# Four pairs instead of two in the long w_down passes, six residues by accumulating DMA, other orders and another rule for loading pairs

## The chip, the core and the metric

The kernel runs on one core of a Trainium2 chip. Its engines run side by side and wait for each other by semaphores: the tensor engine (PE, with its weight loads PEld), VectorE (DVE), ScalarE (ACT), GpSimd (POOL) and SyncE (SP). SP and POOL issue DMA transfers, and each engine takes its instructions in program order. The metric is the device time of one execution in microseconds.

## What is computed

One layer of a hybrid block on 256 rows of 2048 columns, all in float32. The part that matters is the second half, SwiGLU:

```
hn = rms_norm(h, norm2_g)                       # 256 x 2048
a  = hn @ w_gate                                # 256 x 5632
bu = hn @ w_up                                  # 256 x 5632
h  = h + (silu(a) * bu) @ w_down                # 256 x 2048
```

Before it come an input projection, attention, a convolution and an output projection, which the change does not touch.

## The kernel before

**Three products for one.** A float32 product is made of reduced-precision (float32r) ones. Each operand is split into a rounded part ("hi") and a residue ("lo"); a product then takes three matmuls: hi·hi, lo·hi and hi·lo. For a weight tile ACT makes the rounded part (`whi`, line 320) and DVE the residue (`wlo`, line 329). A residue can also be made "by DMA": ACT writes the negated rounded value into `wlo` (line 323), and a DMA issued by POOL adds the raw tile to it (line 324).

**Plain units and pairs.** The hidden width of 5632 is eleven blocks of 512 columns, in groups of 4, 4 and 3 (`FGROUPS`). After the gate and up projections of a group comes its part of the w_down product: a pass over the group's k-tiles (a k-tile is 128 rows of w_down, four to a block) in two halves of 1024 output columns. The work of a half is a list of units, run in the order of a string (`DORDERS`):

- "g" and "u" are plain units: two k-tiles by 512 columns, for both halves of the 256 rows, 12 matmuls (`multiply_two`, lines 1014, 1015, 1020). "g" takes the first 512 columns of the half, "u" the second.
- "s" is a pair unit: k-tile p of the group's first block with k-tile p of its second block, by all 1024 columns. It is a 2x2 block product by seven products instead of eight (Strassen-Winograd), 21 matmuls (`multiply_pair`, lines 993 to 995). It replaces 24 matmuls of plain units.

A pair costs more preparation: DVE forms four sums of the loaded weights (`wt`, lines 966 to 968), ACT rounds the seven matrices (`wh`, lines 969 and 972), and DVE makes their residues (`wlb`, line 975, of the loaded ones; `wlt`, line 976, of the sums). The activations need sums and residues as well (`make_down_forms`), made in between while later blocks run. Before the change two of the four k-tiles of the first two blocks go as pairs (`ND = 2`), in all three groups. The gate and up projections are built of the same units; in each of their blocks four pairs and eight plain units, some of these with the residue by DMA (`BY_DMA`).

**What sets the order.** Nothing is scheduled by a planner: the order of the emitted program is the order on each engine. `run_chunks` walks over all units; at unit t it emits the residues of units up to t + 2, then the loads of pairs that lie up to 6 units ahead (`PAIR_AHEAD`), then the loads and casts of the units up to t + 3 (near a pair) or t + 2, and then the matmuls of t. Generators that were started earlier (transposes, forms, the sums of finished products) go one step further at each `resume()`. All loads are issued by SP, so a load that waits for its buffer holds back every load behind it. Buffers: five for raw tiles (`raw`), three each for `whi` and `wlo`, two for a pair's loaded weights (`wb`), two each for `wh`, `wlb` and `wlt`, one for `wt`. A special rule held for the first four pairs, those of the first gate/up block that has any ("block 1"):

```
behind = [k for k in range(n) if chunks[k].get("kind") == "s"][NS]
...
if p < behind and p > t + hi_lead:
    break
```

So these were loaded no more than three units ahead. The two `wb` buffers hold, until then, the normalized activations `hn`, from which the forms of the gate and up projections are made.

Of the kernel before, what the change touches and what calls it, by code (L numbers as in the profile page):

```python
# [12 lines left out]
F32 = mybir.dt.float32  # L13
# [82 lines left out]

HI_AHEAD, LO_AHEAD = 3, 2

PAIR_AHEAD = 6

FIRSTS = [sum(FGROUPS[: g + 1]) for g in range(len(FGROUPS))]

# [20 lines left out]
def tile_block(  # L123
# [697 lines left out]
    def transposed(j, aa):  # L821
        last = j + 1 in FIRSTS
        b = j - group_of(j)[1]
        for t in range(N // P // 2):

            pool_, tag = (acc_ps, "acc") if last else (aux_ps, "aux")
            pt = pool_.tile([P, 2, S], F32, tag=tag, name="ps_a")
            for i in range(2):
                for m in range(NM):
                    c = (2 * t + i) * P  # L830
                    pe.transpose(pt[:, i, m * P : (m + 1) * P], aa[m][:, c : c + P], ident)  # L831
            if b < 2 and 2 * t < ND:
# [12 lines left out]
            yield from lag(1 if last else 4)  # L845
# [11 lines left out]

    def make_down_forms(g):

        fp = ffn["pool"]  # L860
        gap = lambda: lag(5 if FGROUPS[g] == 4 else 2)
        a11, a21 = (raw_act[0][:, :, m * P : (m + 1) * P] for m in range(NM))
        a12, a22 = (raw_act[1][:, :, m * P : (m + 1) * P] for m in range(NM))

        hi = fp.tile([P, 7, ND, P], F32R, tag="dhi", name="dhi")
        lo = fp.tile([P, 3, ND, P], F32R, tag="dlo", name="dlo")
        fa, fb = (lhs.tile([P, 2, ND, P], F32, tag=t, name="dsums") for t in ("lhi", "llo"))
        act.copy(hi[:, 0], a11)
        dve.scalar_tensor_tensor(fa[:, 0], a21, -1.0, a22, ALU.mult, ALU.subtract)
        yield from gap()  # L870
        act.copy(hi[:, 1], a12)
        dve.scalar_tensor_tensor(fa[:, 1], fa[:, 0], -1.0, a11, ALU.mult, ALU.subtract)
        yield from gap()
        act.activation(hi[:, 2], a22, AF.Copy, scale=-1.0)
        dve.tensor_tensor(fb[:, 0], a11, a21, ALU.subtract)
        yield from gap()
        act.copy(hi[:, 3:5], fa)
        dve.tensor_tensor(fb[:, 1], a12, fa[:, 1], ALU.subtract)
        yield from gap()
        act.copy(hi[:, 5:7], fb)  # L880
        for i, a in ((0, a11), (1, a12)):
            dve.tensor_tensor(lo[:, i], a, hi[:, i].bitcast(F32), ALU.subtract)
            yield from gap()
        dve.scalar_tensor_tensor(lo[:, 2], a22, -1.0, hi[:, 2].bitcast(F32), ALU.mult, ALU.subtract)
        yield from gap()
        pairs = [lhs.tile([P, 2, ND, P], F32R, tag=t, name="dlo2") for t in ("lhi", "llo")]
        for i, f in ((0, fa), (1, fb)):
            dve.tensor_tensor(pairs[i], f, hi[:, 3 + 2 * i : 5 + 2 * i].bitcast(F32), ALU.subtract)
            yield from gap()
        los = [lo[:, 0], lo[:, 1], lo[:, 2], pairs[0][:, 0], pairs[0][:, 1], pairs[1][:, 0], pairs[1][:, 1]]  # L890
        down_forms[g] = {f: (hi[:, i], los[i]) for i, f in enumerate((0, 1, 3, 4, 5, 6, 2))}

    forms = {}
# [176 lines left out]

    def down_pass(g, j0, nb):
        k0 = j0 * HD
        ks = [k for k in range(nb * HD) if k >= 2 * HD or k % HD >= ND]
        twos = [dict(ks=(k0 + a, k0 + b), rows=slice(k0 + a, k0 + b + 1, b - a), k=None)
                for a, b in zip(ks[::2], ks[1::2])]
        for i, order in enumerate(DORDERS[nb]):
            n = 2 * i
            end = {}  # L1080
            fast_block(order, [dict(p=p, rows=slice(k0 + p, k0 + p + HD + 1, HD)) for p in range(ND)], twos,
                       dict(g=(w_down, n * N), u=(w_down, (n + 1) * N)),
                       dict(pairs=lambda: down_forms.get(g), plain=actT.get),
                       lambda sums, n=n, end=end: down_half(g, n, sums, end),
                       lambda sums, n=n, end=end: down_whole(g, n, sums, end))

    halfway = {}

# [158 lines left out]
```

## Time and profile before

| | |
|---|---|
| median of 3 runs | 1048.9 us (1048.76 to 1049.65) |
| the profiled execution | 1048.92 us |
| its span, first to last instruction | 1047.1 us |
| granted clock of the tensor engine | 1.0 |
| first group: w_down pass, first half | 517.1 to 560.3 us |
| first group: w_down pass, second half | 560.3 to 602.5 us |
| second group: w_down pass | 768.7 to 854.2 us |
| block 1 (first block with pairs) | 390.9 to 433.6 us |

The page gives busy times by engine. A matmul's record is longer than the distance to the next one, so rates are read from starts. In a row of groups the number after the bar is the busy time, then the mean in ns, then the idle time of the engine just before these instructions and what ended it. A row "A <- B: x, n, m" of the waits says that A waited for B for x us in total, n times, m us at most. In a timeline row stand start, length, engine, line, operation, tiles, shape and count; SPq is SP's queue of DMA issues, and its length runs to the end of the last issue of the row.

### The profile page before, as it was taken

How to read it: one execution, taken by the hardware profiler on the slowest of the kernel's cores; microseconds unless marked ns; L12 is line 12 of the kernel's file. 1: busy time of each engine (PE TensorE's matmuls, PEld its weight loads, DVE VectorE, ACT ScalarE, POOL GpSimd, SP SyncE). 2: the span in 40 equal slices, each digit the busy share in tenths (PEclk: the TensorE clock that was granted, in tenths of full speed). 3: DMA queues.
4: the chain of work that ended last, by engine and by line, in shares of the span. 5: the costliest groups of instructions: out<-in, count | busy, mean ns of one | idle time of the engine just before them, and what ended most of it. 6: DMA issues, size and time to landing. Idle time of an engine off the chain costs nothing.

```text
span 1047.1 us, 12933 instructions
## 1 busy us (share of the span) xinstructions
PE 1036.2 (99%) x4663; PEld 852.5 (81%) x4663; DVE 900.6 (86%) x1095; ACT 621.6 (59%) x786; POOL 100.5 (10%) x143
## 2 busy tenths in 40 slices
PE   9999999999999999999999999999999999999998
PEld 7888887877788788888888888888888888888886
DVE  7899889898765599999787898999878789989897
ACT  7544666755756565776463657666644446657442
POOL 0130122201100100000001010000000110000010
PEclk9999999999999999999999999999999999999999
DMA  9657654453546566987867789879757879798683
GB/s 335 227 182 280 212 163 167 154 181 134 177 153 226 194 223 214 268 266 236 232 210 188 217 271 273 256 217 285 248 175 241 219 208 291 222 287 267 187 265 85
DMA packets 113936, 231.30 MB, mean 221 GB/s; under 512 B 7504, under 2 KB 8656, under 8 KB 113616
## 3 DMA queue, kind: packets, MB, share of 16 engines
q1 hardware_dynamic: 104864, 203.71, 56.9%
q0 software_dynamic: 8864, 26.74, 13.4%
q8 instruction: 36, 0.59, 0.2%
q14 instruction: 28, 0.23, 0.1%
q10 hardware_dynamic: 144, 0.03, 0.0%
HBM read 204.24 MB, written 9.44 MB: 204 GB/s over the span
## 4 chain that ended last, share of the span: by engine, by line
PE 61%; DMA 2%; DVE 2%; issue 1%; ACT 0%; DVEq 0%; POOLq 0%
PE q L1020 12%; PE q L1014 12%; PE q L1015 12%; PE q L995 8%; PE q L993 7%; PE q L994 7%; DMA raw<-in_w_down_dram 1%; PE ps_a L831 1%; DMA wlo<-raw 1%; PE acc L365 1%; PE acc L359 1%; PE acc L360 1%; DVE wlo L329 1%; DVE wlt L976 0%; DVE wt L966 0%
## 5 line engine op out<-in xcount | busy, mean ns | idle before, releaser
L320 ACT CAST whi<-raw 128x1024 fp32r<-128x1024 f32 (+1 forms) x273 | 281.5, 1048 | 141.6 <-PE acc L360 58.9
L329 DVE TENSOR_TENSOR wlo<-raw,whi 128x1024 fp32r<-128x1024 f32 (+1 forms) x239 | 287.8, 1218 | 73.5 <-ACT whi L320 73.3
L972 ACT CAST wh<-wt 128x2048 fp32r<-128x2048 f32 x52 | 99.6, 1914 | 77.6 <-DVE wt L968 76.9
L976 DVE TENSOR_TENSOR wlt<-wt,wh 128x2048 fp32r<-128x2048 f32 x52 | 119.1, 2290 | 14.9 <-ACT wh L972 14.7
L359 PE MATMUL acc<-whi,xhi 128*128 128x512 f32 x320 | 126.9, 397 | 1.0 <-ACT whi L320 0.9
L360 PE MATMUL acc<-whi,xlo 128*128 128x512 f32 x320 | 125.2, 391 | 0.0
L1014 PE MATMUL q<-whi,chi 128*128 128x512 f32 x320 | 125.2, 391 | 0.0
L1015 PE MATMUL q<-whi,clo 128*128 128x512 f32 x320 | 124.5, 389 | 0.0
L993 PE MATMUL q<-wh,fhi 128*128 128x512 f32 x280 | 109.9, 393 | 0.0
L994 PE MATMUL q<-wh,flo 128*128 128x512 f32 x280 | 109.1, 390 | 0.0
L517 DVE SCALAR_TENSOR_TENSOR y<-upad,cw,y 128x256 f32<-128x256 f32 x240 | 102.2, 482 | 2.2 <-ACT y L510 2.2
L1014 PE MATMUL q<-whi,ahi 128*128 128x512 f32 x256 | 100.2, 391 | 0.0
L1015 PE MATMUL q<-whi,alo 128*128 128x512 f32 x256 | 99.6, 389 | 0.0
L975 DVE TENSOR_TENSOR wlb<-wb,wh 128x1536 fp32r<-128x1536 f32 x52 | 91.1, 1752 | 1.8 <-ACT wh L969 1.8
L365 PE MATMUL acc<-wlo,xhi 128*128 128x512 f32 x320 | 87.8, 396 | 2.0 <-DVE wlo L329 2.0
L1020 PE MATMUL q<-wlo,chi 128*128 128x512 f32 x320 | 85.7, 390 | 0.2 <-DMA wlo<-raw 0.2
L969 ACT CAST wh<-wb 128x1536 fp32r<-128x1536 f32 x52 | 76.6, 1474 | 0.0
L365 PEld LDWEIGHTS acc<-wlo,xhi 128*128 128x128 f32 x320 | 59.7, 189 | 15.3 <-DVE wlo L329 3.3
L359 PEld LDWEIGHTS acc<-whi,xhi 128*128 128x128 f32 x320 | 60.4, 189 | 14.3 <-ACT whi L320 1.9
L1020 PEld LDWEIGHTS q<-wlo,chi 128*128 128x128 f32 x320 | 59.9, 188 | 13.2 <-DMA wlo<-raw 0.8
L360 PEld LDWEIGHTS acc<-whi,xlo 128*128 128x128 f32 x320 | 60.4, 189 | 12.2
L1014 PEld LDWEIGHTS q<-whi,chi 128*128 128x128 f32 x320 | 60.1, 188 | 12.3
(230 smaller groups left out, 1739.1 us busy)
## 6 DMA issues: line engine op xcount, KB each, us to landing
raw<-in_w_in_dram SPq DMA_DIRECT2D x79, 512.0 KB, 4.6
raw<-in_w_down_dram SPq DMA_DIRECT2D x64, 512.0 KB, 7.2
raw<-in_w_gate_dram SPq DMA_DIRECT2D x48, 512.0 KB, 7.5
raw<-in_w_up_dram SPq DMA_DIRECT2D x48, 512.0 KB, 6.2
wb<-in_w_up_dram SPq DMA_DIRECT2D x40, 512.0 KB, 3.7
wb<-in_w_gate_dram SPq DMA_DIRECT2D x40, 512.0 KB, 4.9
wlo<-raw POOLq DMA_DIRECT2D x34, 512.0 KB, 7.1
raw<-in_w_out_dram SPq DMA_DIRECT2D x32, 512.0 KB, 4.2
```

Source lines behind the costliest of these rows:

```text
L320: act.copy(c["hi"], c["raw"])
L329: dve.tensor_tensor(c["lo"], c["raw"], c["hi"].bitcast(F32), ALU.subtract)
L359: pe.matmul(ps[m], xhi[:, ms], hi[:, j, :], start=c["first"] and j == 0, stop=False)
L360: pe.matmul(ps[m], xlo[:, ms], hi[:, j, :], start=False, stop=False)
L365: pe.matmul(ps[m], xhi[:, ms], lo[:, j, :], start=False, stop=c["last"] and j == nk - 1)
L517: dve.scalar_tensor_tensor(y[:, ct, :], src, wk, y[:, ct, :], ALU.mult, ALU.add)
L976: dve.tensor_tensor(lot, c["t"], c["hi"][:, :SUMMED].bitcast(F32), ALU.subtract)
L993: pe.matmul(ps, hi, c["hi"][:, w], start=bool(first), stop=False)
L994: pe.matmul(ps, lo, c["hi"][:, w], start=False, stop=False)
L1014: pe.matmul(ps, xs[i][0][:, ms], hi[:, i, :], start=i == 0 and bool(c["first"].get(qs[m])), stop=False)
L1015: pe.matmul(ps, xs[i][1][:, ms], hi[:, i, :], start=False, stop=False)
L1020: pe.matmul(sum_bank(c, qs[m]), xs[i][0][:, ms], lo[:, i, :], start=False, stop=i == 1 and bool(c["last"].get(qs[m])))
```

## The change

In the passes of the first two groups all four pairs of the first two blocks' k-tiles are taken as pair units (`NDS = (4, 4, 2)`), so that a half has 4 pairs and 8 plain units where it had 2 and 12. Two new orders are written for them. Of the plain units, four in the first half and two in the second have their residue made by DMA. The activation forms get other buffers and are four k-tiles wide; the k-tiles 2 and 3 of the first two blocks are now kept raw for the forms instead of being split. The rule with `behind` goes; in its place the loop stops loading pairs when three lie between the current unit and the one to be loaded, for all pairs of the program. The third group keeps its orders.

```
-ND = 2
-DORDERS = {4: ("gguuggsguugsuu", "sgggugggusuuuu"), 3: ("gguusggsuu", "gggsgsuuuu")}
+NDS = (4, 4, 2)
+DORDERS = {4: ("gguusgsgsusu", "sggsggsuusuu"), 3: ("gguusggsuu", "gggsgsuuuu")}
+DOWN_BY_DMA = {4: (dict(g=(2, 3), u=(2, 3)), dict(g=(1,), u=(1,))), 3: (dict(g=(), u=()),) * 2}

-PAIR_AHEAD = 6
+PAIR_AHEAD, PAIRS = 6, 3

 def run_chunks():
-        behind = [k for k in range(n) if chunks[k].get("kind") == "s"][NS]
...
                 if chunks[p].get("kind") == "s":
-                    if p < behind and p > t + hi_lead:
+                    if sum(c.get("kind") == "s" for c in chunks[t:p]) >= PAIRS:
                         break
                     load_pair(chunks[p])

 def transposed(j, aa):
-            if b < 2 and 2 * t < ND:
-                raw_act[b] = lhs.tile([P, 2, S], F32, tag=("lhi", "llo")[b], name=f"ar{j}")
-                act.copy(raw_act[b], pt)
+            g = group_of(j)[0]
+            nd = NDS[g]
+            if b < 2 and 2 * t < nd:
+                if not b and not t:
+                    raw_act[g] = ffn["pool"].tile([P, 2, nd, S], F32, tag="draw", name="raw_act")
+                act.copy(raw_act[g][:, b, 2 * t : 2 * t + 2, :], pt)
                 yield from lag(3 if last else 6)
-                if b:
-                    start(make_down_forms(group_of(j)[0]))
+                if b and 2 * t + 2 == nd:
+                    start(make_down_forms(g))
                 continue

 def make_down_forms(g):
+        one = lambda tag, dt, name: lhs.tile([P, 4, P], dt, tag=tag, name=name)[:, :nd]
+        hi = [one("lhi", F32R, "dhi") for _ in range(4)]
+        lo = [one("llo", F32R, "dlo") for _ in range(4)]
+        f4, f5, f6, f2 = (one(t, F32, "dsums") for t in ("lhi", "lhi", "llo", "llo"))
...
+        hs = ffn["pool"].tile([P, 2, nd, P], F32R, tag="dhs", name="dhs")
...
+        ls = ffn["pool"].tile([P, 4, nd, P], F32R, tag="draw", name="dls")
+        act.copy(ls[:, 3], f6)
+        for i, (f, h) in enumerate(((f4, hs[:, 0]), (f5, hs[:, 1]), (f6, ls[:, 3]))):
+            dve.tensor_tensor(ls[:, i], f, h.bitcast(F32), ALU.subtract)

 def down_pass(g, j0, nb):
-        ks = [k for k in range(nb * HD) if k >= 2 * HD or k % HD >= ND]
-        twos = [dict(ks=(k0 + a, k0 + b), rows=slice(k0 + a, k0 + b + 1, b - a), k=None)
-                for a, b in zip(ks[::2], ks[1::2])]
+        nd = NDS[g]
+        ks = [k for k in range(nb * HD) if k >= 2 * HD or k % HD >= nd]
+        twos = [dict(ks=(k0 + a, k0 + b), rows=slice(k0 + a, k0 + b + 1, b - a), k=i)
+                for i, (a, b) in enumerate(zip(ks[::2], ks[1::2]))]
...
-                       lambda sums, n=n, end=end: down_whole(g, n, sums, end))
+                       lambda sums, n=n, end=end: down_whole(g, n, sums, end), DOWN_BY_DMA[nb][i])
```

Positions in an order string are counted from 0: in "gguusgsgsusu" the pairs stand at 4, 6, 8 and 10, and the units at 5, 7, 9 and 11 have their residue by DMA. Block 1 runs in the order "gsggsgsuusuu", before and after.

More of the change, by code (lines that the diff above doesn't have):

```diff
@@ L868, in make_down_forms @@
-        act.copy(hi[:, 0], a11)
-        dve.scalar_tensor_tensor(fa[:, 0], a21, -1.0, a22, ALU.mult, ALU.subtract)
+        raw = raw_act.pop(g)
+        a11, a21 = (raw[:, 0, :, m * P : (m + 1) * P] for m in range(NM))
+        a12, a22 = (raw[:, 1, :, m * P : (m + 1) * P] for m in range(NM))
+        one = lambda tag, dt, name: lhs.tile([P, 4, P], dt, tag=tag, name=name)[:, :nd]
+        hi = [one("lhi", F32R, "dhi") for _ in range(4)]
+        lo = [one("llo", F32R, "dlo") for _ in range(4)]
@@ L885, in make_down_forms @@
         yield from gap()
[L886 to L891, printed above, removed]
+        dve.tensor_tensor(lo[3], f2, hi[3].bitcast(F32), ALU.subtract)
@@ L1080, in down_pass @@
             end = {}
-            fast_block(order, [dict(p=p, rows=slice(k0 + p, k0 + p + HD + 1, HD)) for p in range(ND)], twos,
+            fast_block(order, [dict(p=p, rows=slice(k0 + p, k0 + p + HD + 1, HD)) for p in range(nd)], twos,
                        dict(g=(w_down, n * N), u=(w_down, (n + 1) * N)),
```

33 lines of the change are left out of this document (18 added, 15 removed).

## The prediction

> **What bounds the kernel now.** I read the page first, then the waits of the tensor engine (PE), then its timeline, and then the stages around w_down.
>
> ```profile
> span 1047.1 us, 12933 instructions
> PE 1036.2 (99%) x4663; PEld 852.5 (81%) x4663; DVE 900.6 (86%) x1095; ACT 621.6 (59%) x786; POOL 100.5 (10%) x143
> ```
> ```profile
> PE acc L365 <- DVE wlo L329: 2.0, 2, 1.2
> ...
> PE q L1020 <- DMA wlo<-raw: 0.2, 1, 0.2
> ```
>
> PE is in use almost without a break; of the rows of its waits the first shown is the largest: 2.0 us in total, 1.2 at most at a time. So the number of matmuls sets the time, as long as nothing arrives late. A matmul's shown length (0.39 us) overlaps the next one, so its price is read from starts in the timeline:
>
> ```profile
> 409.93 0.39 PE L1014 MATMUL q<-whi,chi 128*128 128x512 f32 x1
> ...
> 412.65 0.39 PE L993 MATMUL q<-wh,fhi 128*128 128x512 f32 x1
> ...
> 417.41 0.39 PE L1014 MATMUL q<-whi,chi 128*128 128x512 f32 x1
> ```
>
> At 409.93 begins a plain unit of 12 matmuls, at 412.65 a pair unit of 21. That is 2.72 / 12 and 4.76 / 21: 0.227 us for each matmul in both.
>
> The windows of two gate/up blocks and of the two w_down passes of the first group show how much room DVE has beside PE:
>
> ```profile
> 433.60:475.40 41.80, 41.80 (x190) 34.60 (x189) 39.60 (x42) 30.59 (x32) 3.44 (x4) 1.00 0.87 257
> 475.40:517.10 41.70, 41.70 (x189) 34.53 (x188) 34.42 (x37) 24.64 (x25) 2.58 (x3) 1.00 0.80 234
> 517.10:560.30 43.20, 43.20 (x195) 35.61 (x194) 37.98 (x36) 23.52 (x22) 0.00 (x0) 1.00 0.63 207
> 560.30:602.50 42.20, 42.20 (x187) 34.91 (x187) 32.96 (x33) 19.74 (x18) 5.25 (x6) 1.00 0.77 204
> ```
>
> Columns: length, then PE, weight loads, DVE, ACT, POOL busy, granted clock, DMA. PE fills every window; in the first, DVE fills 39.60 of 41.80 (95%) and PE still never waits.
>
> **Part 1: fewer matmuls.** A long pass had 2 pairs and 12 plain units, 2 x 21 + 12 x 12 = 186 matmuls; it gets 4 and 8: 180. There are four such passes (two groups, two halves), so 24 matmuls go: 24 x 0.227 = 5.4 us less on the path. The third group keeps its orders and gains nothing.
>
> **Part 2: more work on DVE and ACT.** Prices:
>
> ```profile
> 397.78 1.22 DVE L966 TENSOR_TENSOR wt<-wb 128x1024 f32<-128x1024 f32 x1
> ...
> 400.37 1.75 DVE L975 TENSOR_TENSOR wlb<-wb,wh 128x1536 fp32r<-128x1536 f32 x1
> 402.43 2.29 DVE L976 TENSOR_TENSOR wlt<-wt,wh 128x2048 fp32r<-128x2048 f32 x1 [0.31 <-ACT wh L972]
> ```
> ```profile
> L320 ACT CAST whi<-raw 128x1024 fp32r<-128x1024 f32 x271 | 280.3, 1051 | 141.2 <-PE acc L360 58.9 <-PE q L1015 42.1 <-DMA raw<-in_w_down_dram 22.7
> L329 DVE TENSOR_TENSOR wlo<-raw,whi 128x1024 fp32r<-128x1024 f32 x237 | 286.4, 1222 | 72.9 <-ACT whi L320 72.6 <-PE acc L365 0.2
> ...
> L323 ACT ACTIVATE wlo<-raw 128x1024 fp32r<-128x1024 f32 x34 | 35.9, 1055 | 0.0
> ```
>
> A pair takes DVE from 397.78 to 404.72, less 0.31 idle: 6.6 us (sums 2.6, first residue 1.75, second 2.29). A plain residue is 1.22. First half of a pass: two pairs more (13.2), eight DVE residues fewer (9.8, since four of the eight plain units left go to the DMA): 37.98 + 3.4 = 41.4 us, beside 40.8 of matmuls and 1.0 of transposes (43.20 less 186 x 0.227). Second half: six residues fewer: 32.96 + 13.2 - 7.3 = 38.9 beside 40.8, 95%, about what the window at 433.60 carried for free. The first half alone, at 99%, would not hold: at 95% it needs 43.7, 1.9 us over. Part 4 makes PE stand still for longer than that, so I charge nothing there. At the seam between the halves only one plain unit now lies between the last pair and the next one, and the bank sums of the first half stand on DVE behind that next pair's residues and one plain residue; I charge 0.75 us for each group, between 0 and 2.5 (a residue and two operations of half its size).
>
> The activation forms become 128x512 operations, half a plain residue each, about 0.6 us: eleven of them are at most 6.7 us, less what they replace, in the two blocks before the pass, which leave DVE 2.2 and 7.3 us free. Nothing on the path; if all fell into the first of these blocks, 4.5 us. Six accumulating copies for each group on POOL: it is 10% busy, and their order there is ahead of the half's writes to `hd`. ACT gets two operations for each such unit instead of one, 2.1 us, and is 59% busy. None of this is counted.
>
> **Part 3: where the loads now stand, first block.** SP issues loads in program order and stops at the first that must wait. A pair's load (L956) waits until the `wb` buffer of two pairs earlier is free, which is when DVE has written that pair's `wlb`; every raw tile behind it waits too. The trace shows both the rule and its size:
>
> ```profile
> SPq L956 <- DVE wlb L975: 336.4, 41, 13.4
> ```
> ```profile
> 361.68 10.67 SPq L315 DMA_DIRECT2D raw<-in_w_up_dram  x5
> 377.44 0.37 SPq L956 DMA_DIRECT2D wb<-in_w_up_dram  x1
> ...
> 378.41 6.40 SPq L315 DMA_DIRECT2D raw<-in_w_gate_dram  x3
> ...
> 392.10 0.37 SPq L956 DMA_DIRECT2D wb<-in_w_up_dram  x1
> ...
> 532.61 0.88 SPq L956 DMA_DIRECT2D wb<-in_w_down_dram  x2
> 533.83 16.24 SPq L315 DMA_DIRECT2D raw<-in_w_down_dram  x7
> ```
> ```profile
> 517.99 1.28 DVE L1113 TENSOR_TENSOR sum<-q,sum 128x512 f32<-128x512 f32 x2
> 519.19 1.28 DVE L1115 TENSOR_TENSOR sum<-sum,sum 128x512 f32<-128x512 f32 x2
> 520.39 2.35 DVE L329 TENSOR_TENSOR wlo<-raw,whi 128x1024 fp32r<-128x1024 f32 x2
> ...
> 530.83 1.75 DVE L975 TENSOR_TENSOR wlb<-wb,wh 128x1536 fp32r<-128x1536 f32 x1
> ```
>
> `wlb` ends at 532.58, and SP issues the two halves of the pair at 532.61 and the raw tile 1.2 us after. From a raw tile's issue to its landing, one such tile behind two pair halves took 5.5 us (issued at 601.48), another 7.4 (551.19); then the accumulating copies, near a pass and over the run:
>
> ```profile
> DMA to landing us min/median/max: 5.5/5.5/5.5
> ```
> ```profile
> DMA to landing us min/median/max: 7.4/7.4/7.4
> ```
> ```profile
> DMA to landing us min/median/max: 5.7/6.2/6.7
> ```
> ```profile
> DMA to landing us min/median/max: 5.0/7.1/10.2
> ```
>
> I take 6.4 for a raw tile, the middle of the two, and 6.2 for the copy, since few transfers run beside it at a pass's start, as in that row.
>
> Without `behind`, the loads of block 1's pairs move up in SP's queue. The first pair's load, issued at 377.44 when the second-norm forms let its buffer go, now stands ahead of the last three w_up raw tiles, which the trace issues before 372.4. They get the place of 378.41; with 5.5 the first lands at 383.9, and its cast ends at 385.0. PE wants it here:
>
> ```profile
> 382.39 0.39 PE L359 MATMUL acc<-whi,hhi 128*128 128x512 f32 x1
> ...
> 405.62 0.40 PE L995 MATMUL q<-wlt,fhi 128*128 128x512 f32 x1
> ```
>
> It is 2.6 us late. The tile at position 0 is behind the second pair's load in turn, so block 1's first `wlb`, which released SP at 392.10, comes at about 395.0 (the 2.6 and a little for the casts that are now bunched on ACT). Now the third pair's load waits for it, and behind that stands the raw tile of position 3, which the trace issued within 378.41 + 6.40. It lands at 395.0 + 1.2 + 6.4 = 402.6; cast 1.05, residue 1.22, and then the second pair's 6.9 us on DVE, in that order, end at 411.8. PE uses this `wlt` at 405.62 in the trace: 6.2 us late (5.3 to 7.2 by the two landings). PE has no slack later to win it back.
>
> **Part 4: where the loads now stand, first half of a long pass.** In "gguusgsgsusu" the pair at position 8 needs the buffer of the one at position 4, and its load stands in SP's queue right ahead of the raw tile of position 5, which is one of the tiles split by the accumulating DMA. Let T be the pass's first matmul:
>
> ```profile
> 517.11 0.39 PE L1014 MATMUL q<-whi,ahi 128*128 128x512 f32 x1
> ...
> 528.95 0.39 PE L1014 MATMUL q<-whi,ahi 128*128 128x512 f32 x1
> ```
>
> On DVE the last block's four closing operations run at 517.99 to 520.4, after PE's last matmul of that block; then come one residue (to 521.6), the sums of position 4 (to 524.2), one residue (525.3) and its `wlb` (527.0): T + 9.9. The pair's load and the raw tile follow: landing at T + 9.9 + 1.2 + 6.4 = T + 17.5. Cast and negated copy on ACT take 2.1, the accumulating copy 6.2: T + 25.8. PE, after four plain units and the transposes, starts position 4 at T + 11.8 (528.95), position 5 at T + 16.6, and its second half, which reads this residue, 8 matmuls later at T + 18.4. It stands for 7.4 us. With the ends of the rows (5.5 and 5.0; 7.4 and 7.1) 5.3 to 9.3. ACT, which waits in order for that cast, also delays the pair at position 6, but PE is late by more than that. The raw tile of position 7 follows right behind; those of 9 and 11 wait for the `wlb` of 6 and 8, which by the same steps reach PE in time now that PE is 7 us later. So the stall is paid once a pass: 2 x 7.4 = 14.8 us.
>
> For the accumulating copy, the Trainium skill ("DMA: Bandwidth & Descriptors", Anatomy of one DMA) gives 2.0 us and bytes / 436e3 us for each DMA, which would be an estimated 3.2 us for 512 KB; by it the two stalls would be 6 us shorter together and the time 1060. The trace does not agree: its quickest copy took 5.0.
>
> **Sum.** -5.4 + 6.2 + 14.8 + 1.5 = +17.1 on the profiled execution's 1048.9 (span 1047.1 and 1.8 around it, equal to the median of the three runs): 1066 us. With the low ends -5.4 + 5.3 + 10.6 + 0, 1059; with the high ones -5.4 + 7.2 + 18.6 + 5, 1074.
>
> **Rivals.** *Faster: the loads are far enough ahead.* Then only part 1 counts, 1043.5, or up to 1047 if DVE's 1.9 us in each first half show. For it: the gate/up windows hold the same mix of units without PE idle, and the first raw tile of the first pass is issued 28 us ahead of T:
>
> ```profile
> L315 SPq DMA_DIRECT2D raw<-in_w_down_dram x64: 367/368/1232, 488.7 to 1015.7; - x64
> ```
>
> Against it: the pair stands four units after the load that it blocks there, one unit here. It decides on whether position 5's tile is issued before T + 3.7 (T + 18.4 less 6.4, 2.1 and 6.2); I find it at T + 11.1. Chance 0.09.
>
> *Only one of the two late places is real.* If the passes keep up, the first block's 6.2 eats the gain: 1049.7, chance 0.04. If the first block keeps up, 1060, chance 0.06.
>
> *The standing PE loses its clock.* The first matmuls of the run are twice as far apart:
>
> ```profile
> 1.36 3.89 PE L157 MATMUL ps_warm<-ident 128*128 128x128 f32 x17 [1.36 <-POOL neghalf L151]
> ...
> 5.89 0.63 PE L359 MATMUL acc<-whi,xhi 128*128 128x512 f32 x1
> 6.32 0.63 PE L360 MATMUL acc<-whi,xlo 128*128 128x512 f32 x1
> ```
>
> 0.43 us, not 0.227, up to 5 us after PE's first work at 1.36; the granted clock is 1.00 in every window above, and the longest idle was 1.2 us. If each of the two stalls brought those 5 us at half speed back, each would cost 2.5 us more: 1071. The Trainium skill says so ("TensorE: Matmul & The Clock Gate", HAM oscillation): a gap above about 3.4 us lets the clock fall by half. No run here has such a gap yet. Chance 0.12.
>
> *The chain stays late.* If copies take the 10.2 of the worst row, positions 7 to 11 are late too, some 4 us more in each of the four halves: 1080. Chance 0.07.
>
> **How the numbers follow.** The forecast has 0.62. The range 1055 to 1075 holds its bounds, the clock case and the first-block-keeps-up case. A change of under 0.2% (2.1 us) cannot be told from none here: faster 0.09, same 0.04, slower 0.87.
>
> **What would show it.** The waits view of the new profile should have PE waiting for the copy `wlo<-raw` (second half of a plain unit) for some 5 us twice, with a shorter wait for `whi` ahead of it, and a wait for `whi` and `wlt` of together some 6 us between 380 and 415. The windows of the second halves should be near 41 us, those of the first near 49. SP's wait for `wlb` should end just ahead of position 5's raw tile. Wrong would be a PE without new waits (then the time is near 1044), or waits at the second halves (then DVE is the bound).

## The result, and the profile after

The changed kernel takes 1080.5 us (median of 4 runs, 1080.1 to 1083.1) against 1049.2 before (4 runs on the same chip, 1048.8 to 1049.7): 1.030 times as long, 95% interval 1.0286 to 1.0322. The forecast was 1066, the range 1055 to 1075: the sign was right, the size and the range were not. The profiled execution has a span of 1078.3 us, 31.2 more than before.

The page's head and first line, and the waits of PE ("A <- B: us in total, times, longest"):

```profile
span 1078.3 us, 12936 instructions
PE 1040.1 (96%) x4639; PEld 851.9 (79%) x4639; DVE 925.8 (86%) x1109; ACT 647.5 (60%) x804; POOL 112.6 (10%) x155
```
```profile
PE q L1002 <- DVE alo L844: 14.1, 2, 7.4
PE q L1029 <- DMA wlo<-raw: 6.0, 5, 2.2
PE acc L360 <- ACT whi L321: 4.0, 3, 2.6
PE q L1002 <- ACT sum L1102: 2.3, 2, 1.7
PE acc L366 <- DVE wlo L330: 2.0, 2, 1.2
PE q L1004 <- DVE wlt L985: 1.6, 3, 1.2
```

Before, the largest of these rows was 2.0 us. Now the largest is a wait of a pair's matmul (line 1002) for `alo`, the residue of an activation tile (line 844), which the forecast did not have at all; it stands 14.1 us in two stops, one for each long pass. The second row is the wait that the forecast named, but short and five times.

The windows of the first halves and second halves of the two long passes (length, busy PE, weight loads, DVE, ACT, POOL, granted clock, DMA):

```profile
523.50:577.90 54.40, 44.46 (x189) 35.31 (x187) 41.02 (x35) 30.54 (x27) 3.51 (x5) 0.94 0.70 203
577.90:620.50 42.60, 41.45 (x181) 33.60 (x182) 40.56 (x40) 23.90 (x20) 5.45 (x7) 1.00 0.90 257
786.60:842.40 55.80, 44.65 (x189) 35.42 (x187) 40.89 (x35) 30.39 (x26) 3.45 (x4) 0.94 0.70 205
842.40:885.20 42.80, 42.56 (x181) 35.11 (x182) 40.65 (x40) 24.23 (x20) 5.56 (x7) 0.96 0.88 246
```

The first halves took 43.2 us before and take 54.4 and 55.8; the second halves took 42.2 and take 42.6 and 42.8, so they lose what six matmuls fewer would give (1.4 us) and a little more. The clock, 1.00 in every window before, is 0.94 in both first halves and 0.96 in the last of these windows.

The timeline of the first pass, around the stop (T, the pass's first matmul, is at 523.50):

```profile
533.42 0.88 SPq L965 DMA_DIRECT2D wb<-in_w_down_dram  x2
...
534.35 1.33 SPq L316 DMA_DIRECT2D raw<-in_w_down_dram  x2
...
537.84 0.39 PE L1004 MATMUL q<-wlt,dhi 128*128 128x512 f32 x1
...
542.39 1.05 ACT L321 CAST whi<-raw 128x1024 fp32r<-128x1024 f32 x1 [9.84 <-DMA raw<-in_w_down_dram]
543.35 1.05 ACT L324 ACTIVATE wlo<-raw 128x1024 fp32r<-128x1024 f32 x1
544.30 0.57 ACT L842 CAST ahi<-ps_a 128x512 fp32r<-128x512 f32 x1
...
544.90 0.69 DVE L844 TENSOR_TENSOR alo<-ps_a,ahi 128x512 fp32r<-128x512 f32 x1 [6.12 <-ACT ahi L842]
...
545.65 0.80 PE L1002 MATMUL q<-wh,dhi 128*128 128x512 f32 x1 [7.42 <-DVE alo L844]
...
546.24 0.63 PE L1003 MATMUL q<-wh,dlo 128*128 128x512 f32 x1
...
546.67 0.63 PE L1004 MATMUL q<-wlb,dhi 128*128 128x512 f32 x1
```

Read from the top: SP issues the load of the pair at position 8 at 533.42, T + 9.9, and the raw tile of position 5 right behind. ACT, with nothing to do for 9.84 us, waits for this tile in order. Behind the tile's cast and negated copy in ACT's queue stands `ahi`, the rounded copy of the second transposed tile of the group's last block; only after it can DVE make `alo`, and only then is the PSUM bank of that transposed tile (`ps_a`) free. The last block's transposed tiles share a pool of banks with the sums of the pairs, and the 13th matmul of the pair at position 4 is the first into that bank. So PE stops in the middle of the pair at position 4, one unit before the place where the late tile is used. And after the stop the matmuls start 0.43 us apart (546.24, 546.67), not 0.227.

Where the 31.2 us are, from the lengths of the units in the trace: 24 matmuls fewer, -5.4; block 1 (the second block with pairs begins at 440.0, before at 433.6), +6.4; the pair at position 4, 14.2 and 13.7 us long instead of 4.9, +18.1 (stops of 7.4 and 6.6, slower matmuls 1.9 and 2.1); waits for accumulated residues at positions 7 and 11, +6.3; the first pair of the second halves (the seam), +6.0. The sum is 31.4, within 0.2 of what was measured. A unit's length here runs from the start of its first matmul to the end of its last.

### The profile page after: what moved, and what is told of

It reads as the page before. It is cut to its first block, busy times and chain, and to the rows that moved or that the text cites. A ratio compares the mean times of both kernels' runs of the same rounds, so it can differ in the third digit from the quotient of the medians.

```text
span 1078.3 us, 12936 instructions
## 1 busy us (share of the span) xinstructions
PE 1040.1 (96%) x4639; PEld 851.9 (79%) x4639; DVE 925.8 (86%) x1109; ACT 647.5 (60%) x804; POOL 112.6 (10%) x155
## 5 line engine op out<-in xcount | busy, mean ns | idle before, releaser
L321 ACT CAST whi<-raw 128x1024 fp32r<-128x1024 f32 (+1 forms) x257 | 265.7, 1050 | 148.1 <-PE acc L361 58.1
L330 DVE TENSOR_TENSOR wlo<-raw,whi 128x1024 fp32r<-128x1024 f32 (+1 forms) x211 | 255.1, 1220 | 57.5 <-ACT whi L321 56.9
L981 ACT CAST wh<-wt 128x2048 fp32r<-128x2048 f32 x60 | 115.1, 1918 | 95.5 <-DVE wt L977 95.4
L985 DVE TENSOR_TENSOR wlt<-wt,wh 128x2048 fp32r<-128x2048 f32 x60 | 137.5, 2291 | 17.7 <-ACT wh L981 17.2
L984 DVE TENSOR_TENSOR wlb<-wb,wh 128x1536 fp32r<-128x1536 f32 x60 | 105.2, 1753 | 5.2 <-ACT wh L978 5.1
L325 POOL DMA_DIRECT2D wlo<-raw x46 | 39.8, 865 | 541.8 <-ACT wlo L324 406.5
L978 ACT CAST wh<-wb 128x1536 fp32r<-128x1536 f32 x60 | 88.4, 1474 | 0.3 <-ACT wlo L324 0.2
L1023 PE MATMUL q<-whi,ahi 128*128 128x512 f32 x192 | 75.3, 392 | 0.0
L1024 PE MATMUL q<-whi,alo 128*128 128x512 f32 x192 | 74.8, 389 | 0.0
L975 DVE TENSOR_TENSOR wt<-wb 128x1024 f32<-128x1024 f32 x60 | 73.2, 1221 | 0.2
```

The lines of the kernel that those rows point to most:

```text
L321: act.copy(c["hi"], c["raw"])
L330: dve.tensor_tensor(c["lo"], c["raw"], c["hi"].bitcast(F32), ALU.subtract)
L981: act.copy(c["hi"][:, :SUMMED], c["t"])
L985: dve.tensor_tensor(lot, c["t"], c["hi"][:, :SUMMED].bitcast(F32), ALU.subtract)
L1023: pe.matmul(ps, xs[i][0][:, ms], hi[:, i, :], start=i == 0 and bool(c["first"].get(qs[m])), stop=False)
L1024: pe.matmul(ps, xs[i][1][:, ms], hi[:, i, :], start=False, stop=False)
```

## The experiments

The theory: the root is the order of SP's queue. A pair's load that must wait for its buffer stands ahead of the raw tile that is needed a unit later; that brings the first block's 6.4 us and, through ACT's queue and a PSUM bank, the stops at position 4. The rivals: the accumulating transfers are the root; the bank held by the transposed tile is the cause by itself; the pairs' work on VectorE is. All runs are listed with their times at the end of this section.

**The rule alone.** The kernel before, with the new rule for pair loads and nothing else of the change:

```
-        behind = [k for k in range(n) if chunks[k].get("kind") == "s"][NS]
...
-                    if p < behind and p > t + hi_lead:
+                    if sum(c.get("kind") == "s" for c in chunks[t:p]) >= 3:
```

> The kernel before with one edit: the rule by which a pair's load may be taken ahead is the changed kernel's (at most three pairs from the present unit on), in place of the one that held the first block's pairs back; orders, pairs and residues are those of before. Theory (the loads' order in SP's queue costs the first block its delay, the new pairs nothing there): only the first of the fast gate-and-up blocks changes, by the +6.4 us that the changed kernel shows there, so 1049.2 + 6.4 = about 1055.5, with the stop of 2.6 us near 385 us in it. Rival (that block is late by something else of the change): 1049, no stop there.

It took 1054.7 us beside 1048.2 of the kernel before on that chip: +6.4. The waits of PE in its profile:

```profile
PE acc L359 <- ACT whi L320: 3.6, 3, 2.6
PE q L994 <- DVE wlt L975: 2.0, 3, 1.6
```

These are the two waits that part 3 of the prediction named, for the cast of the last w_up tiles and for `wlt`. And the other way round, the removed rule put back into the changed kernel (beside the new one):

```
+        behind = [k for k in range(n) if chunks[k].get("kind") == "s"][NS]
...
                     if sum(c.get("kind") == "s" for c in chunks[t:p]) >= PAIRS:
                         break
+                    if p < behind and p > t + hi_lead:
+                        break
```

> The changed kernel with the removed rule put back beside PAIRS = 3: the first fast block's pairs are loaded no further ahead than in the kernel before; the passes are those of the changed kernel. Theory: the first block's 6.4 us go and the passes keep all of theirs, 1080.5 - 6.4 = 1074. Rival (the delay of that block gave loads of the passes time, so that part of it comes back there): between 1074 and 1080.

1074.6 us in one run, 5.9 less than the changed kernel (beside the kernel before on their own chips, +26.3 against +31.3, it is 5.0); the passes kept their stops (6.93 and 6.98 us inside the pair at position 4). The first block's loss belongs to the rule, and most of it adds to the rest.

**Pair loads one pair later.** The changed kernel with one number changed:

```
-PAIR_AHEAD, PAIRS = 6, 3
+PAIR_AHEAD, PAIRS = 6, 2
```

> The changed kernel with PAIRS = 2 for 3: the same products, orders and residues, and a pair's load waits in the program until only two pairs are ahead of it, which puts the load of the pair at position 8 of a long pass's first half behind the raw tiles of positions 5 and 7 in SP's queue. Theory (the head of SP's queue is the root): the stop inside the pair at position 4 and its half clock go, 9.3 and 8.8 us, and of the later waits (6.3 at positions 7 and 11, 5.8 at the seam) some or all; of the first block's 6.4 us the first 2.6 stay. So 1080.5 - 18.1 - (0 to 12.1) - (0 to 3.8) = 1046 to 1062, most likely about 1051. Rivals: if the accumulating transfers are the root, or the larger load on VectorE, little goes: 1074 or more, since neither is changed.

1058.3 us, ratio to before 1.0094 (1.0077 to 1.0111): of the 31.3 us lost 10.1 are left. The time lies in the expected range, above the likely 1051. Its waits:

```profile
PE acc L360 <- ACT whi L321: 4.5, 3, 2.6
PE q L1029 <- DMA wlo<-raw: 2.8, 3, 1.3
PE q L1002 <- DVE alo L844: 2.3, 2, 1.2
PE q L1002 <- DVE sum L1108: 2.1, 2, 1.0
```

The residues by transfer, their number, the pairs and the orders are as in the changed kernel; only the place of pair loads among the raw tiles in SP's queue differs, and the wait for `alo` falls from 14.1 to 2.3 us. This is the root of the stops. In the first block half of the loss stays (3.2 of 6.4: the second block with pairs begins at 436.8), with its 2.6 us for the cast, because the first pair's load still stands ahead of the last w_up tiles.

**The bank.** Where the transposed tiles of the last block are copied, two lags are set to 0, so that `ahi` and `alo` stand ahead of position 5's cast:

```
-            yield from lag(1 if last else 2)
+            yield from lag(0 if last else 2)
...
-            yield from lag(1 if last else 4)
+            yield from lag(0 if last else 4)
```

> The changed kernel with the two lags between the transposed tiles of a group's last block set to 0: both rounded copies of these tiles then stand on ScalarE ahead of the cast of position 5's raw tile, so their PSUM bank is free for the pair at position 4; SP's queue, orders and residues are as in the changed kernel. Theory (the raw tile's late landing is the root, the bank only where TensorE meets it): the pair at position 4 runs its 4.9 us, and position 5 then waits, about 3.2 us for its cast and 4.1 us for its residue, 7.3 together in place of the stop of 7.4; what the half clock costs (about 2 a group) may go or stay: 1076 to 1081. Rival (the bank held by the transposed tile is the cause by itself): both stops go, 2 x 9 less: 1062.

1080.8 us (one run): no change. Its waits show where the stop went:

```profile
PE q L1029 <- DMA wlo<-raw: 10.2, 6, 3.8
PE q L1023 <- ACT whi L321: 5.8, 2, 3.0
PE q L1004 <- DVE wlt L985: 5.6, 7, 1.6
```

With the bank free, PE gets through position 4 and stands at position 5 instead, 3.03 us for its cast and 2.54 for its accumulated residue in the first group, 2.79 and 3.83 in the second. The bank is only where PE met the late tile first; the rival of the bank is refuted. This kernel has the stop at the very place that the prediction gave for it.

**No accumulating transfers in the passes.**

```
-DOWN_BY_DMA = {4: (dict(g=(2, 3), u=(2, 3)), dict(g=(1,), u=(1,))), ...
+DOWN_BY_DMA = {4: (dict(g=(), u=()), dict(g=(), u=())), ...
```

> The changed kernel with all residues of the long passes on VectorE instead of six of a pass by accumulating transfer; loads and orders are unchanged. Theory: the stop inside the pair at position 4 stays in both groups (18.1 us with the clock), since nothing of SP's queue or of ScalarE's casts ahead of it is changed; the waits for accumulated residues at positions 7 and 11 (6.3 us) go, and the residues on VectorE cost between nothing and the same again: 1072 to 1082. Rival (the accumulating transfers are the root of the passes' loss): nearly all of 18.1 + 6.3 + 5.8 goes: 1052 to 1058.

1078.8 us (one run). The stop at position 4 is longer, not gone:

```profile
PE q L1002 <- DVE alo L844: 19.6, 2, 9.9
```
```profile
542.62 1.22 DVE L330 TENSOR_TENSOR wlo<-raw,whi 128x1024 fp32r<-128x1024 f32 x1 [7.52 <-ACT whi L321]
543.76 1.22 DVE L975 TENSOR_TENSOR wt<-wb 128x1024 f32<-128x1024 f32 x1
...
546.35 0.68 DVE L844 TENSOR_TENSOR alo<-ps_a,ahi 128x512 fp32r<-128x512 f32 x1
```

Position 5's residue is now on DVE, and it and the sums of the next pair stand ahead of `alo` there. The waits at positions 7 and 11 are gone, as expected. The transfers are not the root.

**Both rules, and what is left.** PAIRS = 2 with the removed rule put back (the two diffs above together) has no pair load ahead of a raw tile needed sooner:

> PAIRS = 2 and the removed rule together: no pair's load stands ahead of a raw tile needed sooner, neither in the first block nor at position 8. The run with PAIRS = 2 alone had its second fast block begin at 436.8 against 433.6 before, so 3.2 us of its 1058.3 should go: 1055.1. That leaves the passes 85.4 - 88.1 = 2.7 us slower than before in the first group, with waits of 1.2 for the transposed tile, 1.3 for position 5's residue and 1.5 at the seam. Rival: SP's queue accounts for those as well, and they go with it: 1046.

1054.6 us, ratio 1.0061 (1.0046 to 1.0076), as expected from the first block's 3.2. Yet it is 6.3 us over the kernel before, and 24 matmuls fewer should have put it 5.4 below: 11.7 us are still lost, in the passes. Its first pass and its waits:

```profile
516.50:562.50 46.00, 42.74 (x190) 34.16 (x188) 40.54 (x36) 30.60 (x27) 3.68 (x5) 1.00 0.76 218
562.50:604.90 42.40, 41.38 (x182) 33.54 (x181) 40.48 (x40) 23.68 (x19) 5.26 (x7) 1.00 0.92 263
```
```profile
PE q L1032 <- DMA wlo<-raw: 4.0, 4, 1.2
PE q L1005 <- DVE alo L847: 2.4, 2, 1.2
...
PE q L1005 <- DVE sum L1111: 2.0, 2, 1.0
```

By the lengths of the units in its trace, 3.0 of these 11.7 us are at the pair at position 4, which waits for `alo`; 5.2 at the accumulated residues of positions 5 and 7; and 3.6 at the seam. The last row names DVE for the seam, but DVE itself stands idle there, in the first pass:

```profile
559.92 1.05 ACT L321 CAST whi<-raw 128x1024 fp32r<-128x1024 f32 x1 [2.79 <-DMA raw<-in_w_down_dram]
...
561.84 0.57 ACT L1105 COPY sum<-q 128x512 f32<-128x512 f32 x1
...
562.43 0.69 DVE L1107 TENSOR_TENSOR sum<-q,sum 128x512 f32<-128x512 f32 x1 [2.79 <-ACT sum L1105]
```

ACT's copy that opens the sums of the first half (line 1105) stands behind the cast and the negated copy of the second half's first accumulated unit (position 2), and that cast waits 2.79 us for its raw tile. DVE's sums start when the copy is done, and the second half's first pair waits for them.

All further kernels are this one with one edit more each, or two. The next ones take these waits away one by one. First the lags of the transposed tiles at 0, as above:

> PAIRS = 2, the removed rule, and the two lags between the last block's transposed tiles set to 0. Now that no raw tile is late, the bank held by the transposed tile is what stops the pair at position 4 (1.2 us and about 0.3 of slower matmuls in each group): that goes, and the pair's own second residue may be late instead, as in the changed kernel with these lags at 0 (0.95 a group). 1055.1 - 3.0 + (0 to 1.9) = 1052 to 1054. Rival (VectorE is full, 40.5 us busy in a half whose matmuls take 40.8, so a wait removed is given back at the next place): 1055.

1056.1 us. The wait for `alo` is gone; in its place stand the pair's own residue (`wlt`, 0.9 us in each group) and longer waits for transfers (2.1 and 1.3 at position 5). Then, in addition, the residue of position 5 on VectorE and that of position 3 by transfer (`g=(3,), u=(1, 2, 3)`):

> As the run before, and of the four accumulated residues of a first half the one at position 5 is made on VectorE, the one at position 3 by accumulating transfer instead, so VectorE and the queues have as much to do. The wait of 1.3 and 1.2 us for position 5's transfer goes if that transfer's length is what counts: 2.5 less than the run before, about 1050. Rival (VectorE is full): the residue of position 5 is late on VectorE instead, 1052 to 1055.

1056.2 us: the transfer of position 7 is now late, by 2.0 and 2.1. Then the seam, with the first halves in another order (`"gguusgsgsusu"` to `"ggusgsgsusuu"`), without and with the lags at 0, and with the two measures before together:

> PAIRS = 2, the removed rule, and another order for the first halves, ggusgsgsusuu in place of gguusgsgsusu: each pair one position earlier, two plain units behind the last pair in place of one, so the sums of the half have 5.4 us before the second half's first pair as in the kernel before, in place of 2.7. The seam's waits (1.0 and 1.3 us, with some 0.5 of slower matmuls each) should go: 1054.6 - 3 = 1051.5. Against it: the first pair now meets the transposed tiles one unit sooner, so up to 2.7 us more there in each group, 1057.

> The order of the run before with the two lags of the transposed tiles at 0, so that their copies and residues stand ahead of the first pair's. Seam waits gone and no wait for the transposed tile: 1056.1 - 3 = 1053, down to 1050 if the pair's own residues now come in time; if VectorE is the limit and the time is only given back elsewhere, 1055 to 1056.

> The order ggusgsgsusuu with the lags at 0, and the accumulated residue of the unit behind the first pair (which was 3.0 and 2.7 us late in that run) on VectorE, a later one by transfer in its place. 1056.9 - 5.7 = 1051 if that transfer was the last wait; if VectorE is the limit, its 1.22 us make the next pair's residue late, 1054 to 1056.

1057.4, 1057.0 and 1059.8 us. In the first of them the seam's waits do go, and the second halves run in 40.8 us, which is what their 180 matmuls take (180 x 0.227). In this order the copy that opens the sums stands ahead of the accumulated unit's cast on ACT (558.96 and 562.18). But the first pair meets the transposed tiles sooner (waits of 0.42, 2.11 and 1.54 us inside it). With the lags at 0 this turns into 2.95 and 2.67 us for the transfer of the unit behind that pair, and with this residue on VectorE into waits for `wlt` and the next transfers (by the trace of an execution of 1063.2 us; the other three took 1059.7 to 1059.9). A plain unit between the two halves instead (`"sggsggsuusuu"` to `"gsggsgsuusuu"`):

> PAIRS = 2, the removed rule, and the second halves in the order gsggsgsuusuu for sggsggsuusuu: a plain unit stands between the last pair of a first half and the first of the second, 2.7 us more for VectorE there. But its first product goes to a bank that the sums free fifth of six, not first. If VectorE's load of pairs is what makes the seam late: the seam's 2.0 to 2.3 us go, 1052. If the sums' own chain is: the plain unit waits instead, about 1.5 to 3 a group, 1055 to 1058.

1063.8 us: its first product needs a bank that the sums free fifth, and waits 3.93 and 3.60 us; the rival of the sums' own chain, and more than its 1.5 to 3. Fewer and more transfers:

> PAIRS = 2 and the removed rule as before (1054.6), and all residues of the long passes on VectorE. What is left of the loss in the passes is 2.4 us at the transposed tiles, 4.0 for accumulated residues and 2.0 to 2.3 at the seams. If VectorE is the limit of the first halves (40.5 us busy, 90% and more of the stretch from position 2 to 8), four residues of 1.22 us more there and two in a second half make each pass longer by up to 7.3: 1054.6 - 4.0 + (5 to 14.6) = 1056 to 1065. If the accumulating transfers are what is left, their 4.0 go and nothing takes their place: about 1050.5.

> The other way: six of the eight residues of a first half by accumulating transfer (of the first of each stream and the rest), two fewer for VectorE, 2.4 us a half. If VectorE is the limit: between 1054.6 and 1050. If the transfers are: the two new ones are late too, or make the others so, 1056 or more.

> The same with the whole computation: PAIRS = 2, the removed rule, position 5's residue on VectorE, three transfers in a first half. The late transfer goes (1.1 and 1.2 us, with its slower matmuls 3 in all), VectorE gets 1.22 us more in each first half. If the two limits stand behind each other: 1054.6 - 3 + (2.4 to 5) = 1054 to 1056.5. If the transfer alone is the limit there: 1051.5.

1058.0 us with none, 1055.3 with six in a first half (one run) and 1057.1 with three. Each residue put back on VectorE costs time and the two transfers more gain nothing. In the last of the three the wait for `alo` is 2.33 and 2.34 us, twice what it was, since position 5's residue stands ahead of it on VectorE.

So a wait removed came back elsewhere, and often dearer: six of these nine kernels came out above every value that was expected of them (1056.1, 1056.2, 1057.0, 1059.8, 1063.8 and 1057.1). Two kernels take work off VectorE instead. In the w_down passes the residues of three of the four sums of a pair are left out (another residue of the pair is multiplied in their place, so PE has as much to do):

```
+        if c["from"]["u"][0] is w_down:
+            n = 1
+            dve.tensor_tensor(lot[:, :n], c["t"][:, :n], c["hi"][:, :n].bitcast(F32), ALU.subtract)
+            c["lo"] = [lot[:, 0]] + [lob[:, i] for i in range(3)] + [lob[:, i] for i in range(7 - SUMMED)]
+            return
```

> PAIRS = 2 and the removed rule; in the w_down passes the residues of three of the four sums of a pair are not computed (the product takes another residue of the pair in their place), so VectorE's largest operation falls from 2.29 us to about 0.7, some 6 to 8 us less in each first half and each second half; ScalarE, the transfers, the orders and TensorE's work are unchanged. If VectorE is the limit of the passes: the waits at the transposed tile, at the seam and for residues whose neighbours it held up go, 1054.6 - (6 to 10) = 1045 to 1049. If the order or the transfers are: 1052 to 1055.

1052.2 us (one run). Its first pass, and the only waits of its passes:

```profile
516.80:563.70 46.90, 43.68 (x189) 35.64 (x189) 34.99 (x39) 31.77 (x27) 4.33 (x5) 0.96 0.76 210
563.70:604.50 40.80, 40.80 (x181) 33.78 (x180) 34.27 (x37) 22.71 (x18) 4.92 (x6) 1.00 0.94 279
```
```profile
PE q L1037 <- DMA wlo<-raw: 6.6, 2, 3.4
```

The waits at the transposed tile and at the seam are gone, and the second half is at the 40.8 us of its matmuls. But now position 5's transfer alone, 3.22 and 3.40 us late with slower matmuls behind it, takes most of it back. The time falls where the rival put it (1052 to 1055), but the waits say that both have a part: with less work on VectorE `alo` is in time, and the transfer is the next limit, 2.4 us behind. For the seam this kernel shows less, since PE also reaches it later, behind the stop at position 5. Both away, that is, this kernel with position 5's residue on VectorE (`g=(3,), u=(2, 3)`):

> The run with less work on VectorE (three of the four residues of a pair's sums left out in the w_down passes), and position 5's residue of a first half on VectorE instead of by accumulating transfer. If VectorE and that transfer are all of what is left: 1052.2 - 2 x (3.3 + 1.6) = 1042.4, between 1042 and 1045, below the kernel before; that is a bound, since part of the computation is left out. If something else is left: 1048 or more.

1049.5 us, ratio 1.0013 (1.0003 to 1.0022), where 1042 to 1045 was expected. Its waits:

```profile
PE q L1037 <- DMA wlo<-raw: 3.3, 3, 1.7
PE acc L366 <- DVE wlo L330: 2.0, 2, 1.2
PE acc L360 <- ACT whi L321: 1.8, 2, 1.2
PE q L1010 <- DVE sum L1116: 1.7, 2, 0.9
PE q L1010 <- DVE alo L847: 1.5, 2, 0.7
```

The two rows on `acc` are of stages ahead of the passes. 5.1 of the 11.7 us are gone with both. Of the rest, position 7's transfer is 1.67 and 1.45 us late, and the one residue put back on VectorE, which stands there ahead of the second `alo`, is enough to make `alo` late again.

The seam's wait is not VectorE's: counted from the first pass's first matmul, the copy that opens the sums comes at 43.8 us in both of these kernels, but PE reaches the second half at 46.9 us in the first of them and at 44.8 in this one. DVE again stands idle for that copy (3.35 us), and the cast ahead of it waits 2.10 us for its raw tile.

So two limits are shown by runs: VectorE's work at the transposed tile, and the accumulating copies, which took 7.2 to 10.5 us to land in the passes of the version with 1054.6 and the first of the two kernels with less work. The third, the raw tile and the cast ahead of the sums on ACT, is read from the traces; the order `ggusgsgsusuu`, in which the copy stands ahead of that cast, had no wait for the sums, but it also has a plain unit more there. That these three are all of the 11.7 follows from the lengths in one trace and not from a run: no kernel here was without all of them. No version that computes everything beat the kernel before; the best, with 1054.6, is 0.6% slower.

All runs, in us (the kernel before had medians of 1048.1 to 1048.3 beside them):

| kernel | time | runs |
|---|---|---|
| the rule alone in the kernel before | 1054.7 | 1 |
| changed, removed rule put back | 1074.6 | 1 |
| changed, lags 0 | 1080.8 | 1 |
| changed, no transfers in the passes | 1078.8 | 1 |
| changed, PAIRS = 2 | 1058.3 | 4 |
| **PAIRS = 2 and removed rule** (all below are this with an edit) | 1054.6 | 4 |
| lags 0 | 1056.1 | 4 |
| lags 0, transfer at 3 for 5 | 1056.2 | 4 |
| order ggusgsgsusuu | 1057.4 | 4 |
| the same, lags 0 | 1057.0 | 4 |
| the same, lags 0, the early transfer later | 1059.8 | 4 |
| second halves gsggsgsuusuu | 1063.8 | 4 |
| no transfers | 1058.0 | 4 |
| six transfers in a first half | 1055.3 | 1 |
| three transfers in a first half | 1057.1 | 4 |
| fewer residues of the pairs (not the whole computation) | 1052.2 | 1 |
| the same, position 5 on VectorE (not the whole computation) | 1049.5 | 10 |

## Why the prediction was right and wrong

- **Part 1, 5.4 us for 24 matmuls: right.** A unit's length outside the stops is unchanged, and the second halves reach 40.8 us once nothing is late (shown in the runs with the other order and with less work on VectorE).
- **Part 3, the first block, 6.2: right in its place and its mechanism; the total in part by luck.** 6.4 in the trace, 6.4 by the rule alone, 5.0 to 5.9 by putting the old rule back. The 2.6 us for the late cast at 385 is in it, to the tenth. The second pair's `wlt` let PE go on at 410.70, 5.1 us behind the 405.62 of before, where 6.2 was worked out; the other 1.3 us came behind it, mostly at the next pair's residue (0.5) and at an accumulated copy (0.7), which part 3 did not have. Behind the stop of 2.6 us the matmuls were slower as well, by 1.7 us in all; as PE would have waited for that `wlt` in any case, this did not add to the 5.1.
- **Part 4, the queue: right.** SP issues the pair at position 8 at T + 9.9, and position 5's raw tile right behind, as worked out. The raw tile took 8.0 us to land, not 6.4, the copy 4.6, not 6.2; the two errors cancel, which is luck.
- **Part 4, the place of the stop: wrong.** The step that failed is the sentence on ACT, that it "also delays the pair at position 6, but PE is late by more than that". It followed ACT's queue to the next pair's casts and passed over the `ahi` that stands between, on which the bank of the pair at position 4 hangs. This moved the stop a unit forward. That its size, 7.4 and 6.6, came out near the 7.4 that was forecast is luck: the forecast's stop ended with the accumulating copy at T + 25.8, this one ends with `alo` at T + 22.1, and no copy is in it. The run with the lags at 0 shows that this is no cause of its own: the stop at position 5 costs as much.
- **The clock: wrong to leave it a rival.** A stop of 7.4 us was in the forecast itself, and the only rows on slow matmuls were those behind an idle PE. It was given a chance of 0.12; it came in both groups, at 1.9 and 2.1 us of the 2.5 charged there. The rule of the Trainium skill ("TensorE: Matmul & The Clock Gate", HAM oscillation) that was named beside that rival pointed the right way, and the trace agrees: 0.43 us between matmuls after a stop of 7.42.
- **"The stall is paid once a pass": wrong, 6.3 us.** The copies of positions 7 and 11 took 10.0 and 9.8 us to land in the first group and PE lost 1.73 and 0.94 there, 1.15 and 2.45 in the second. Part 4 took the 6.2 that was measured where few transfers ran beside them; here the DMA engines are 70% busy over the half, and 88% or more from 550 on. That this load is what made the copies longer is likely, but no run shows it alone. The rival "the chain stays late" had this step, with a chance of 0.07. That its time of 1080 is the measured one is luck: it charged some 4 us in each of four halves for the copies, where the first halves lost 2.7 and 3.6, and left out the clock and the seam.
- **The seam: 0.75 a group charged, 2.4 and 3.6 measured.** What part 2 passed over is ACT. The copy that opens the sums (line 1102) stands there behind the cast and the negated copy of the second half's first accumulated unit, and that cast waits for a late raw tile (2.19 us of idle ACT in the first group, 2.89 in the second), while DVE stands idle (3.44 and 4.14 us). The forecast looked for the delay in DVE's queue. In the second group slower matmuls are part of the 3.6. The high end of 2.5 was too low there as well.
- **Part 2, nothing charged to VectorE beside PE's own stop: hidden, not settled, by the stop.** Part 2 put a full VectorE at 1.9 us in a first half, and let the stop hide it. Without the stops the wait for `alo`, which goes when VectorE has less to do, costs 1.5 us in each first half, so this size was near. Of the other 8.8 us that the best version loses it had 1.5, the charge for the seams; the accumulated residues (5.2) and the rest of the seams (3.6 in all) it had not. For the second halves part 2's "carried for free" held: they reach 40.8 us once the seam does not wait.

In sum: 0.2 too little for the first block, 3.3 for the stops with their clock, 6.3 for the later copies and 4.5 for the seams make 14.3, within 0.2 of the 14.1 by which the forecast fell short of the profiled execution's increase. The range missed because it held either the terms at their bounds (1074) or the clock (1071), and left the later copies to a rival outside it; the runs show late tile, clock, copies and seam to come together, as one chain.

## What to carry to other kernels

When a load moves up in an in-order queue, follow what is held up through every engine's queue to the first buffer that something earlier needs; a late tile can stop the matmuls before the place where it is used. Where a second engine has nearly as much work as the first (here 40.5 us on VectorE beside 40.8 of matmuls), do not count a removed wait as gained before a run without that engine's work shows what stands behind it. When a wait names an engine that stands idle itself, follow that engine's own wait: at the seam it led from VectorE to ScalarE and to a raw tile. And where a forecast contains a stop of several us, the slower clock behind it belongs in the same term.

## What the runs showed of the hardware

The clock fell after stops much shorter than the longest forecast. Matmuls of the version with PAIRS = 2, the removed rule and the lags at 0, behind a stop of 2.09 us:

```profile
538.76 1.95 PE L1032 MATMUL q<-wlo,ahi 128*128 128x512 f32 x4 [2.09 <-DMA wlo<-raw]
540.50 0.63 PE L1005 MATMUL q<-wh,dhs 128*128 128x512 f32 x1
540.93 0.63 PE L1006 MATMUL q<-wh,dls 128*128 128x512 f32 x1
```

They start 0.43 us apart, for about 3.4 us in all. The first block of the changed kernel shows the same behind a stop of 2.60 us:

```profile
385.17 0.74 PE L360 MATMUL acc<-whi,hhi 128*128 128x512 f32 x1 [2.60 <-ACT whi L321]
385.71 0.63 PE L361 MATMUL acc<-whi,hlo 128*128 128x512 f32 x1
386.14 0.63 PE L360 MATMUL acc<-whi,hhi 128*128 128x512 f32 x1
```

After stops of 1.07 and 1.67 us they kept 0.227. After 2.32 us both were seen, in the two groups of one run without transfers: a pair of 8.47 us and one of 7.58, where 4.92 and the stop make 7.24. And at the second seam of the changed kernel a stop of 1.75 us was followed by it, with one of 2.15 us about 3 us ahead of it. So it is not the length of one stop alone that decides; what else does was not tried. The section of the Trainium skill named above gives about 3.4 us of idle time; here less than two thirds of it (2.09 us) was enough at times, and the measurement decides.
